# A hybrid decoder layer: two slabs of the first stage share a buffer, the squares are added in another order, and the table of slots is set anew

## The chip, the core and the metric

The kernel runs on one core of one Trainium2 chip. The core has TensorE (PE, matrix products; PEld is its load of the stationary operand), VectorE (DVE), ScalarE (ACT), GpSimd (POOL) and SyncE (SP, which here only issues DMAs). Each engine takes its own instructions in order and waits on semaphores for the others. The metric is the device time of one execution in microseconds, as the median of three runs.

## The reference, cut to what matters

The layer has 256 tokens of width 1024, in float32. It normalises x, projects it with one matrix, feeds two mixers (8 heads of block attention, 4 heads of a gated delta rule), and projects the result back onto x:

```
h    = rms_norm(x, norm_w)                         # mean of squares over 1024
proj = h @ w_in                                    # q,k,v,z of attention; qkv, z, b, a of the delta rule
qa, ka = rms_norm(heads(q_a)), rms_norm(heads(k_a))
y_a  = attention(qa, ka, v_a, rel_bias) * silu(z_a)
q_d, k_d, v_d = split(silu(causal_conv(qkv_dn)));  q_d, k_d = l2_norm(q_d), l2_norm(k_d)
g, beta = -exp(a_log) * softplus(a_dn + dt_bias), sigmoid(b_dn)
y_d  = rms_norm(gated_delta_rule_chunked(q_d, k_d, v_d, g, beta)) * silu(z_dn)
out  = x + concat(y_a, y_d) @ w_out
```

## The kernel before, in words

**Products.** Every large product is done in three passes: a float32 weight slab is split into a rounded part `wh` (ScalarE, line 188) and a rest `wl` (VectorE, line 189), x likewise into `xh` and `xl` (lines 259 and 260), and TensorE adds wh·xh, wh·xl and wl·xh (lines 249 to 251, 738 to 740, 827 to 829). The weights come as 44 slabs: z0 to z7 (128x520, the first stage), d0 to d11 (128x1024, inputs of the delta rule), then 16 slabs a (attention) and 8 slabs o (output). A slab is loaded by `load()` into one of four rotating buffers `wr` and split by `split()` into one of four `wh` and four `wl`. `chunk(i)` issues loads up to slab i+7 and splits up to slab i+4. All loads of slabs and of x (`px`, line 201) are issued by SP, in the order of the program.

**First stage.** Slab zk meets row block k of x; for each k there are two steps of six products. The mean of squares that the norm needs is made beside this in `norm()`: four squares of two row blocks each, `sq0` to `sq3` (ScalarE, line 269), added on VectorE (lines 274 and 276), then two small products with ones (line 279), which stand in TensorE's order between the two steps of k = 6. The result goes through `mtok` (line 281) and POOL (line 282) to `rtok`, for which the gates of the delta rule wait (line 302).

**Order of the work.** TensorE's order is the order in which the program is written: `products()` is the main stream, and after each of its steps `advance()` counts up by one and lets every other stream whose slot has come emit its next piece. The table `AT` holds these slots: ("base0", 1): 103 means that the second piece of stream base0 is emitted when the count is 103. The order on DVE, ACT, POOL and SP is made by a scheduler from priorities and its own estimate of the times, so a new slot moves instructions there too. The streams: `bias` (attention bias), `norm`, `gates`, `prep0` and `prep2` (delta rule heads, transposes L429, products L453 and L469), `base0` and `base1` (a triangular inverse: VectorE steps L498 and L500, transposes L503 and L507, products from L520 on), `scan0` to `scan3`, `heads..` (q and k of attention, L636 to L660), `pair0` to `pair3` (softmax of two heads: logits L680, maximum L687, exponential L123, division L698, transposes L703, values L714 and L716). L123 is the line of a helper that ScalarE's activations share, L135 that of the reciprocal root on POOL.

Of the kernel before, what the change touches and what calls it, by code (L numbers as in the profile page):

```python
# [8 lines left out]
F32 = mybir.dt.float32  # L9
F32R = mybir.dt.float32r  # L10
AF = mybir.ActivationFunctionType
ALU = mybir.AluOpType
AX = mybir.AxisListType

P = 128
S = 256
D = 1024
KT = 8
# [7 lines left out]
ZC = 520  # L26
# [8 lines left out]
LD, LS, PRI, REP, MTL, BDK = 7, 4, 100, 16, 1, 14  # L35
OUTS = ((0, 2), (0, 0), (1, 2), (1, 0), (0, 3), (1, 3), (0, 1), (1, 1))
AT = {
    ("attention", 0): 89, ("attention", 1): 92, ("attention", 2): 128, ("attention", 3): 113, ("attention", 4): 129,
# [3 lines left out]
    ("base1", 8): 124, ("bias", 0): 0, ("bias", 1): 3, ("bias", 2): 43, ("gates", 0): 24, ("gates", 1): 35,  # L42
# [13 lines left out]
}  # L56
SEGS = (2, 0, 1, 3)
# [4 lines left out]
def tile_hymba_layer(ctx: ExitStack, tc: tile.TileContext, xt, wz, wdn, wat, wout, rb, cst, oneh, out):  # L62
    nc = tc.nc
    PE, ACT, DVE, POOL = nc.tensor, nc.scalar, nc.vector, nc.gpsimd
# [4 lines left out]
    wp = ctx.enter_context(tc.tile_pool(name="wp", bufs=4))  # L69
# [4 lines left out]
    def new(shape, name, dt=F32):  # L74
        return cp.tile(shape, dt, name=name, tag=name)

    def rot(shape, name, tag, bufs=2, dt=F32):
        return rp.tile(shape, dt, name=name, tag=tag, bufs=bufs)
# [55 lines left out]
    def rsqrt(y, m):  # L134
        POOL.tensor_tensor(out=y, in0=m, in1=mhalf.to_broadcast(list(m.shape)), op=ALU.pow)  # L135
# [13 lines left out]
    for _ in range(NWARM):  # L149
# [11 lines left out]
    WB = 1024  # L161
# [1 line left out]
              + [(f"d{i}", wdn[i], 1024) for i in range(12)]  # L163
              + [(f"a{s}{i}", wat[4 * s + i], 1024) for hf in range(2) for s in SEGS for i in (2 * hf, 2 * hf + 1)]
              + [(f"o{mh}{n}", wout[4 * mh + n], 1024) for mh, n in OUTS])
    raws, halves, loads = [], [], []

    def parts(i, n):
        return [slice(0, n)] if i else [slice(0, S), slice(S, n)]

    def load():
        if len(raws) < len(chunks):
            name, src, n = chunks[len(raws)]
            t = wp.tile([P, WB], F32, name=f"wr_{name}", tag="wr", bufs=4)
            for r in parts(len(raws), n):
                i = nc.sync.dma_start(t[:, r], src[:, r])
            raws.append(t)
            loads.append(i)
# [13 lines left out]
    def chunk(i):  # L192
        while len(raws) < min(i + LD, len(chunks)):
            load()
        while len(halves) < min(i + LS, len(chunks)):
            split()
        return halves[i]

    for k in range(KT):
        r = slice(P_COLS + k * S if k else 0, P_COLS + (k + 1) * S)  # L200
        nc.sync.dma_start(px[:, r], xt[:, r])
        load()
# [60 lines left out]
    def norm():  # L263
        ps = yield from grab1()
        for i in range(4):
            sq = rot([P, 2, S], f"sq{i}", "k2", 4)
            xi = x[:, 2 * i:2 * i + 2, :]
            if i in SQA:
                ACT.activation(sq, xi, AF.Square)
            else:  # L270
                POOL.tensor_tensor(out=sq, in0=xi, in1=xi, op=ALU.mult)
            sqs.append(sq)
        for i, j in ((0, 1), (2, 3), (0, 2)):
            DVE.tensor_tensor(out=sqs[i], in0=sqs[i], in1=sqs[j], op=ALU.add)
        sq = sqs[0]
        DVE.tensor_tensor(out=sq[:, 0, :], in0=sq[:, 0, :], in1=sq[:, 1, :], op=ALU.add)
        yield W_NORM
        for c in range(2):
            PE.matmul(ps[:, c:c + 1], lhsT=sqs[0][:, 0, c * P:(c + 1) * P], rhs=ones[:, 0:1], start=True, stop=True)
        m = new([P, 2], "mtok")  # L280
        DVE.tensor_scalar(out=m, in0=ps[:, 0:2], scalar1=1.0 / D, scalar2=EPS, op0=ALU.mult, op1=ALU.add)
        rsqrt(rtok, m)
        done["rtok"] = 1
        POOL.tensor_scalar(out=rhalf, in0=rtok, scalar1=0.5, scalar2=None, op0=ALU.mult)
        POOL.tensor_scalar(out=emt, in0=m, scalar1=EPS, scalar2=None, op0=ALU.mult)
        yield W_NORM2
        for c in range(2):
            PE.matmul(ps[:, S + c * P:S + (c + 1) * P], lhsT=rtok[:, c:c + 1].to_broadcast([P, P]), rhs=ident, start=True,
                      stop=True)
        ACT.copy(rbc, ps[:, S:])  # L290
        free.append(ps)
        table[2] = 1
        convs()
    sqs = []
# [110 lines left out]
    def convs():  # L405
        while early and table[2]:
            conv(*early.pop(0))
# [326 lines left out]
    def products():  # L734
# [11 lines left out]
        for k in range(KT):  # L746
            xsplit(k)
            w = chunk(k)
            if k == CSK:
                after(nc.sync.dma_start(cs, cst[:, 0:3, :]), loads[KT - 1])  # L750
            if k == NS:
                start("norm", norm())
                advance()
            for c in range(2):
                gemm(zb[2][:, c * S:(c + 1) * S], (xh, xl), w, k, c, slice(0, S), k == 0 and c == 0, k == KT - 1 and c == 1)
            yield
            for c in range(2):
                gemm(zb[c][:, :264], (xh, xl), w, k, c, slice(S, ZC), k == 0, k == KT - 1)
            yield
# [96 lines left out]
    def grab1():  # L856
        while not free:
            yield
        return free.pop(0)
# [67 lines left out]
```

## Time and profile before

| | us |
|---|---|
| median of three runs | 168.35 (168.16 to 170.61) |
| the profiled execution, its own time | 168.06 |
| its span, first to last instruction | 166.3 |
| mean granted TensorE clock | 0.996 |
| TensorE busy | 156.0 (94%) |
| VectorE busy | 131.0 (79%) |
| ScalarE busy | 103.6 (62%) |

The parts of the page give busy times by engine, the span in 40 slices, DMA queues, the chain of work that ended last, and the costliest groups by line. A row of the timeline is: start, duration, engine, line, operation, output<-inputs, shape, count, and in brackets the idle time before it with what ended it. A row of the windows view gives for one stretch each engine's busy time, the granted clock, the busy share of the DMA engines and GB/s.

### The profile page before, as it was taken

Reading aid. Unit: us, or ns where it says so; the run is one execution under the profiler, and the core shown is the slowest. Engines: PE = TensorE matmul, PEld = TensorE weight load, DVE = VectorE, ACT = ScalarE, POOL = GpSimd, SP = SyncE. Lnnn points to the kernel's source line nnn. Section 1 sums busy time; section 2 is a strip of 40 time slices with the busy share of each in tenths; the row PEclk is TensorE's granted clock in tenths of the full one; section 3 lists DMA queues with packets and bytes.
Section 4 is the critical chain, followed back from the end, with each engine's and each line's share of the span. In section 5 each row is a group of like instructions: output and inputs, shape, how many; then the busy total and the mean of one; then the engine's idle time right before and its main releaser. Section 6 shows DMA issues by size and latency. Waiting matters only on the chain.

```text
span 166.3 us, 4037 instructions
## 1 busy us (share of the span) xinstructions
PE 156.0 (94%) x1548; PEld 146.8 (88%) x1548; DVE 131.0 (79%) x380; ACT 103.6 (62%) x244; POOL 21.1 (13%) x29
## 2 busy tenths in 40 slices
PE   7799699989999999999998999999999979999990
PEld 7589699989999999999997879988988857999990
DVE  2579689999399999989998999898675997357261
ACT  5688498538997468686645596744666885342200
POOL 7200160000002000033041001031121000003000
PEclk9999999999999999999999999999999999999998
DMA  5998988899746047674343433334223300000033
GB/s 131 278 328 248 342 283 249 253 205 187 312 140 236 7 167 238 229 229 158 126 124 128 132 126 126 132 130 130 54 84 118 126 0 0 4 0 0 4 126 126
DMA packets 9930, 25.01 MB, mean 150 GB/s; under 512 B 1165, under 2 KB 3981, under 8 KB 9912
## 3 DMA queue, kind: packets, MB, share of 16 engines
q1 hardware_dynamic: 9208, 23.66, 46.2%
q10 hardware_dynamic: 576, 0.92, 1.5%
q8 instruction: 12, 0.20, 0.5%
q0 software_dynamic: 128, 0.18, 0.4%
q14 instruction: 6, 0.05, 0.1%
HBM read 23.52 MB, written 1.25 MB: 149 GB/s over the span
## 4 chain that ended last, share of the span: by engine, by line
PE 55%; DVE 19%; ACT 10%; DMA 6%; issue 5%; SPq 2%; POOL 2%; ACTq 0%; DVEq 0%
PE ps L249 5%; PE ps L827 5%; PE ps L829 5%; PE ps L828 5%; PE ps L251 4%; PE ps L250 4%; PE ps L739 4%; PE ps L738 4%; PE ps L740 4%; DVE wl_d L189 3%; DMA px<-xt 3%; DMA wr_z<-wz 2%; DVE wl_a L189 2%; PE ps L703 2%; ACT wh_d L188 2%
## 5 line engine op out<-in xcount | busy, mean ns | idle before, releaser
L249 PE MATMUL ps<-wh_a,xh 128*128 128x256 f32 x96 | 28.4, 296 | 0.0
L738 PE MATMUL ps<-xh,wh_d 128*128 128x256 f32 x96 | 27.7, 289 | 0.0
L739 PE MATMUL ps<-xl,wh_d 128*128 128x256 f32 x96 | 26.8, 279 | 0.0
L740 PE MATMUL ps<-xh,wl_d 128*128 128x256 f32 x96 | 26.8, 279 | 0.0
L250 PE MATMUL ps<-wh_a,xl 128*128 128x256 f32 x96 | 26.7, 278 | 0.0
L251 PE MATMUL ps<-wl_a,xh 128*128 128x256 f32 x96 | 26.7, 278 | 0.0
L188 ACT CAST wh_a<-wr_a 128x1024 fp32r<-128x1024 f32 x16 | 16.8, 1052 | 8.8 <-PE ps L739 6.6
L189 DVE TENSOR_TENSOR wl_a<-wr_a,wh_a 128x1024 fp32r<-128x1024 f32 x16 | 19.5, 1221 | 0.7 <-ACT sqa L636 0.3
L398 DVE SCALAR_TENSOR_TENSOR cv<-un,px,cv 128x255 f32<-128x255 f32 (+2 forms) x36 | 16.8, 476 | 2.5 <-ACT cv L396 2.5
L827 PE MATMUL ps<-yh,wh_o 128*128 128x256 f32 x64 | 18.8, 293 | 0.0
L249 PEld LDWEIGHTS ps<-wh_a,xh 128*128 128x128 f32 x96 | 18.1, 188 | 0.7 <-issue 0.5
L250 PEld LDWEIGHTS ps<-wh_a,xl 128*128 128x128 f32 x96 | 18.1, 189 | 0.1
L738 PEld LDWEIGHTS ps<-xh,wh_d 128*128 128x128 f32 x96 | 18.1, 188 | 0.1
L739 PEld LDWEIGHTS ps<-xl,wh_d 128*128 128x128 f32 x96 | 18.0, 188 | 0.1
L251 PEld LDWEIGHTS ps<-wl_a,xh 128*128 128x128 f32 x96 | 18.1, 188 | 0.0
L740 PEld LDWEIGHTS ps<-xh,wl_d 128*128 128x128 f32 x96 | 18.0, 187 | 0.0
L829 PE MATMUL ps<-yh,wl_o 128*128 128x256 f32 x64 | 17.9, 279 | 0.0
L828 PE MATMUL ps<-yl,wh_o 128*128 128x256 f32 x64 | 17.9, 279 | 0.0
L189 DVE TENSOR_TENSOR wl_d<-wr_d,wh_d 128x1024 fp32r<-128x1024 f32 x12 | 14.7, 1221 | 1.8 <-ACT wh_d L188 1.8
L188 ACT CAST wh_d<-wr_d 128x1024 fp32r<-128x1024 f32 x12 | 12.7, 1056 | 4.1 <-DMA wr_d<-wdn 2.5
L189 DVE TENSOR_TENSOR wl_o<-wr_o,wh_o 128x1024 fp32r<-128x1024 f32 x8 | 9.8, 1221 | 4.5 <-ACT wh_o L188 4.4
L827 PEld LDWEIGHTS ps<-yh,wh_o 128*128 128x128 f32 x64 | 12.0, 188 | 0.5 <-issue 0.3
(209 smaller groups left out, 404.6 us busy)
## 6 DMA issues: line engine op xcount, KB each, us to landing
wr_a<-wat SPq DMA_DIRECT2D x16, 512.0 KB, 3.4
wr_d<-wdn SPq DMA_DIRECT2D x12, 512.0 KB, 5.5
wr_o<-wout SPq DMA_DIRECT2D x8, 512.0 KB, 3.3
wr_z<-wz SPq DMA_DIRECT2D x7, 260.0 KB, 4.1
T<-bd SPq DMA_DIRECT2D x8, 128.0 KB, 6.3
px<-xt SPq DMA_DIRECT2D x7, 128.0 KB, 4.0
out_t<-ot ACTq DMA_DIRECT2D x3, 256.0 KB, 2.4
cs<-cst SPq DMA_DIRECT2D x1, 192.0 KB
```

The costliest lines, as they stand in the source:

```text
L188: ACT.copy(h[:, r], raw[:, r])
L189: eng.tensor_tensor(out=l[:, r], in0=raw[:, r], in1=h[:, r].bitcast(F32), op=ALU.subtract)
L249: PE.matmul(ps, lhsT=xa, rhs=wh[:, cols], start=first, stop=False)
L250: PE.matmul(ps, lhsT=xb, rhs=wh[:, cols], start=False, stop=False)
L251: PE.matmul(ps, lhsT=xa, rhs=wl[:, cols], start=False, stop=last)
L398: DVE.scalar_tensor_tensor(out=a[:, 3 - j:], in0=src[:, 0:S - 3 + j], scalar=pr[:, o + j:o + j + 1], in1=a[:, 3 - j:], op0=ALU.mult, op1=A ...
L738: PE.matmul(ps, lhsT=w[0][:, wk], rhs=xh[:, k, :], start=first, stop=False)
L739: PE.matmul(ps, lhsT=w[0][:, wk], rhs=xl[:, k, :], start=False, stop=False)
L740: PE.matmul(ps, lhsT=w[1][:, wk], rhs=xh[:, k, :], start=False, stop=last)
L827: PE.matmul(ps, lhsT=w[0][:, o], rhs=yh[:, k, :], start=(first and j == 0 and (m % 2 == 0 or alone)), stop=False)
L828: PE.matmul(ps, lhsT=w[0][:, o], rhs=yl[:, k, :], start=False, stop=False)
L829: PE.matmul(ps, lhsT=w[1][:, o], rhs=yh[:, k, :], start=False, stop=(last and j == 1 and (m % 2 == 1 or alone)))
```

## The change

Three edits. In `load()`, the slabs z0 to z7 go in pairs into one buffer (z0 and z1, z2 and z3, and so on), so that the eight take the four buffers once and none has to wait until an earlier one is split. In `norm()`, the three sums of 512 columns and one of 256 become two of 512 and three of 256: `sq0` takes `sq1` and `sq2` whole, is then folded to 256 columns, and takes the two halves of `sq3` one by one. And 52 of the 95 entries of `AT` have other numbers; of this table one line stands here.

```diff
-    ("norm", 0): 13, ("norm", 1): 12, ("norm", 2): 18, ("pair0", 0): 101, ("pair0", 1): 112, ("pair0", 2): 118,
+    ("norm", 0): 13, ("norm", 1): 14, ("norm", 2): 18, ("pair0", 0): 101, ("pair0", 1): 112, ("pair0", 2): 118,
...
-    raws, halves, loads = [], [], []
+    raws, halves, loads, slabs = [], [], [], []
...
-            t = wp.tile([P, WB], F32, name=f"wr_{name}", tag="wr", bufs=4)
+            i = len(raws)
+            if i < KT:
+
+                if i % 2 == 0:
+                    slabs.append(wp.tile([P, 2 * ZC], F32, name=f"wr_{name}", tag="wr", bufs=4))
+                t = slabs[-1][:, i % 2 * ZC:(i % 2 + 1) * ZC]
+            else:
+                t = wp.tile([P, WB], F32, name=f"wr_{name}", tag="wr", bufs=4)
...
-        for i, j in ((0, 1), (2, 3), (0, 2)):
-            DVE.tensor_tensor(out=sqs[i], in0=sqs[i], in1=sqs[j], op=ALU.add)
+
         sq = sqs[0]
-        DVE.tensor_tensor(out=sq[:, 0, :], in0=sq[:, 0, :], in1=sq[:, 1, :], op=ALU.add)
+        for j in (1, 2):
+            DVE.tensor_tensor(out=sq, in0=sq, in1=sqs[j], op=ALU.add)
+        for o in (sq[:, 1, :], sqs[3][:, 0, :], sqs[3][:, 1, :]):
+            DVE.tensor_tensor(out=sq[:, 0, :], in0=sq[:, 0, :], in1=o, op=ALU.add)
```

On SP, in the first stage, before: the loads of z4 to z7 (`wr_z`), the blocks of x between them, and the first slabs d. The brackets name the semaphores waited for; DMAHW0 to DMAHW7 are those of the eight DMAs issued before.

```order
L176 DMA wr_z_112<-wz 128x520 [waits DMAHW2_49,DVE_49]
L201 DMA px<-xt 128x256 [waits DMAHW3_49]
L176 DMA wr_z_115<-wz 128x520 [waits DMAHW4_49,DVE_49]
L201 DMA px<-xt 128x256 [waits DMAHW5_49]
L176 DMA wr_z_118<-wz 128x520 [waits DMAHW6_49,DVE_49]
L201 DMA px<-xt 128x256 [waits DMAHW7_49]
L176 DMA wr_z_121<-wz 128x520 [waits DMAHW0_49,DVE_49]
L750 DMA cs<-cst 128x384 [waits DMAHW1_49]
L176 DMA wr_d_221<-wdn 128x1024 [waits DMAHW2_49,DVE_49]
```

The same place now (lines are those of the changed file):

```order
L183 DMA wr_z_110<-wz 128x520 [waits DMAHW2_49]
L208 DMA px<-xt 128x256 [waits DMAHW3_49]
L183 DMA wr_z_110<-wz 128x520 [waits DMAHW4_49]
L208 DMA px<-xt 128x256 [waits DMAHW5_49]
L183 DMA wr_z_115<-wz 128x520 [waits DMAHW6_49]
L208 DMA px<-xt 128x256 [waits DMAHW7_49]
L183 DMA wr_z_115<-wz 128x520 [waits DMAHW0_49]
L183 DMA wr_d_215<-wdn 128x1024 [waits DMAHW1_49,DVE_49]
L759 DMA cs<-cst 128x384 [waits DMAHW2_49]
```

The waits for VectorE are gone from z4 to z7; a wait for the landing of the eighth DMA before stays in every row. Slab d0 goes ahead of the constants `cs`.

On VectorE, the end of the first stage before (`xl` the rest of x, `wl_z5` to `wl_z7` the rests of slabs, `sq` the sums of squares, `mtok` the scaled mean):

```order
L189 TENSOR_TENSOR wl_z5_224<-wr_z5_115,wh_z5_223 128x520
L260 SCALAR_TENSOR_TENSOR xl_124<-px_96,xh_123 128x256
L189 TENSOR_TENSOR wl_z6_245<-wr_z6_118,wh_z6_244 128x520
L274 TENSOR_TENSOR sq2_304<-sq2_304,sq3_306 128x512
L189 TENSOR_TENSOR wl_z7_265<-wr_z7_121,wh_z7_264 128x520
L274 TENSOR_TENSOR sq0_300<-sq0_300,sq2_304 128x512
L276 TENSOR_TENSOR sq0_300<-sq0_300 128x256
L189 TENSOR_TENSOR wl_d0_285<-wr_d0_221,wh_d0_284 128x1024
```

And now:

```order
L283 TENSOR_TENSOR sq0_296<-sq0_296,sq2_300 128x512
L267 SCALAR_TENSOR_TENSOR xl_120<-px_96,xh_119 128x256
L196 TENSOR_TENSOR wl_z5_218<-wr_z4_110,wh_z5_217 128x520
L285 TENSOR_TENSOR sq0_296<-sq0_296 128x256
L196 TENSOR_TENSOR wl_z6_241<-wr_z6_115,wh_z6_240 128x520
L285 TENSOR_TENSOR sq0_296<-sq0_296,sq3_302 128x256
L196 TENSOR_TENSOR wl_z7_261<-wr_z6_115,wh_z7_260 128x520
L285 TENSOR_TENSOR sq0_296<-sq0_296,sq3_302 128x256
L196 TENSOR_TENSOR wl_d0_281<-wr_d0_215,wh_d0_280 128x1024
```

Behind `wl_z7` stood two dependent sums, of 512 and of 256 columns; now one of 256 stands there. (Rows of `xl` that only repeat are left out.)

On VectorE, the end of base0's steps before (`Mt` and `tm` its serial steps, `Mp` and `MT` its result, `Lb` the start of base1, `qn` and `zs` of attention, `wl_a` the rest of a slab):

```order
L646 TENSOR_TENSOR qn_1311<-ps_77,r_1309 128x512
L500 TENSOR_TENSOR Mt_155<-Mt_155,tm_852 128x2x2x2
L805 TENSOR_TENSOR zs_1364<-ps_76,rbc 128x512
L498 TENSOR_TENSOR tm_852<-Lb_850,Mt_155 128x4
L189 TENSOR_TENSOR wl_a_1372<-wr_a_1195,wh_a_1371 128x1024
L487 STREAM_TRANSPOSE Lb_1324<-pk_1319 128x512
L500 TENSOR_TENSOR Mt_155<-Mt_155,tm_852 128x2x2
L498 TENSOR_TENSOR tm_1326<-Lb_1324,Mt_156 128x2x15
L503 STREAM_TRANSPOSE Mp_883<-Mt_155 128x4x4x8
L500 TENSOR_TENSOR Mt_156<-Mt_156,tm_1326 128x2x15
L507 STREAM_TRANSPOSE MT<-Mp_883 32x4x32 x2
```

And now:

```order
L655 TENSOR_TENSOR qn_1341<-ps_78,r_1339 128x512
L509 TENSOR_TENSOR Mt_151<-Mt_151,tm_859 128x2x2x2
L507 TENSOR_TENSOR tm_859<-Lb_857,Mt_151 128x4
L814 TENSOR_TENSOR zs_1361<-ps_76,rbc 128x512
L509 TENSOR_TENSOR Mt_151<-Mt_151,tm_859 128x2x2
L496 STREAM_TRANSPOSE Lb_1277<-pk_1272 128x512
L512 STREAM_TRANSPOSE Mp_890<-Mt_151 128x4x4x8
L196 TENSOR_TENSOR wl_a_1369<-wr_a_1204,wh_a_1368 128x1024
L507 TENSOR_TENSOR tm_1279<-Lb_1277,Mt_152 128x2x15
L516 STREAM_TRANSPOSE MT<-Mp_890 32x4x32 x4
L509 TENSOR_TENSOR Mt_152<-Mt_152,tm_1279 128x2x15
```

The split `wl_a` that stood ahead of `Mp` now stands behind it. On TensorE the first products of base0 (L520) move with this, from 12 products behind the logits of pair0 and pair1 (L680) to 6 ahead of them. Other moves on TensorE that the prediction speaks of: the product of the bias (L372) goes from after 18 products of the first stage to after 36; the first transposes of prep0 (L429) go 24 products later; one L453 and one L469 of prep2 trade places with products of the main stream; near the end the logits of pair3 (L680) go ahead of the transposes of pair2 (L703).

More of the change, by code (lines that the diff above doesn't have):

```diff
@@ L37 @@
 AT = {
-    ("attention", 0): 89, ("attention", 1): 92, ("attention", 2): 128, ("attention", 3): 113, ("attention", 4): 129,
[3 rows of a table removed]
-    ("base1", 8): 124, ("bias", 0): 0, ("bias", 1): 3, ("bias", 2): 43, ("gates", 0): 24, ("gates", 1): 35,
[12 rows of a table removed]
+    ("attention", 0): 88, ("attention", 1): 97, ("attention", 2): 128, ("attention", 3): 117, ("attention", 4): 120,
[3 rows of a table added]
+    ("base1", 8): 124, ("bias", 0): 0, ("bias", 1): 6, ("bias", 2): 43, ("gates", 0): 29, ("gates", 1): 35,
[12 rows of a table added]
     ("scan3", 5): 211,
```

28 rows, old and new, of the table AT are left out of this document.

## The prediction

> **What bounds the kernel now.** I began with the page's first part and then asked who waits for whom on TensorE.
>
> ```profile
> PE 156.0 (94%) x1548; PEld 146.8 (88%) x1548; DVE 131.0 (79%) x380; ACT 103.6 (62%) x244; POOL 21.1 (13%) x29
> ...
> PE ps L703 <- DVE pb L698: 1.6, 3, 1.0
> PE ps L279 <- DVE sq L276: 1.4, 1, 1.4
> PE ps L654 <- DVE qn L646: 0.8, 1, 0.8
> PE ps L249 <- ACT wh_z L188: 0.7, 2, 0.4
> PE ps L354 <- DVE eD L347: 0.5, 1, 0.5
> ```
>
> TensorE is busy 156.0 of 166.3 us. The change takes no product away, so all it can save is idle time, and the five waits above (us in total, times, longest) sum to 5.0 us. More than 3 us is hard to reach: each wait would have to go without another coming. The second longest, 1.4 us, lies in the stage that the change names. The chain of waits around it:
>
> ```profile
> 11.69 3.98 DMA wr_z<-wz
> ...
> 15.77 0.64 ACT wh_z L188
> ...
> 17.14 0.61 DVE sq L274
> ...
> 17.77 0.44 DVE sq L276
> ```
>
> Columns are start and duration. The load of z7 is issued at 11.69 and lands at 15.7; then come its split on ScalarE and VectorE, two dependent sums of squares, and only then the product L279, for which the rest of TensorE's queue (half of k = 6, all of k = 7, the d slabs) stands in line. TensorE's rows there:
>
> ```profile
> 16.54 0.28 PE L251 MATMUL ps<-wl_z,xh 128*128 128x256 f32 x1
> 18.25 0.61 PE L279 MATMUL ps<-ones,sq 128*128 128x1 f32 x4 [1.43 <-DVE sq L276]
> ```
>
> Products start 0.12 us apart, so TensorE could have gone on at 16.66: 1.6 us are lost here.
>
> Later stages have another limit. In the windows view (stretch, length, then PE, PEld, DVE, ACT, POOL busy):
>
> ```profile
> 26.00:40.00 14.00, 13.45 (x116) 13.25 (x115) 14.00 (x41) 8.02 (x14) 0.00 (x0) 1.00 0.92 220
> ...
> 50.00:85.00 35.00, 35.00 (x294) 34.62 (x292) 33.94 (x98) 24.24 (x60) 4.12 (x3) 1.00 0.49 165
> ```
>
> From 26 to 40 VectorE is never idle, and from 50 to 85 TensorE and VectorE both are full. So a saving of TensorE's at 18 us lasts only if VectorE, too, gets ahead; if it doesn't, TensorE waits longer where it waits for VectorE now, at L354, L654 and L703.
>
> **The change part by part: the first stage.** ScalarE's and VectorE's rows from 10 us on, all back to back, give what each step occupies (start to next start):
>
> ```profile
> 10.76 0.50 ACT L259 ACTIVATE xh<-px 128x256 fp32r<-128x256 f32 x1
> 11.17 0.46 ACT L375 COPY V<-ps 8x384 f32<-8x384 f32 x1
> 11.53 0.62 ACT L188 CAST wh_z<-wr_z 128x520 fp32r<-128x520 f32 x1
> 12.05 0.63 ACT L269 ACTIVATE sq<-px 128x512 f32<-128x512 f32 x1
> 12.59 0.49 ACT L259 ACTIVATE xh<-px 128x256 fp32r<-128x256 f32 x1
> ...
> 10.58 0.48 DVE L260 SCALAR_TENSOR_TENSOR xl<-px,xh 128x256 fp32r<-128x256 f32 x1
> 10.97 0.69 DVE L189 TENSOR_TENSOR wl_z<-wr_z,wh_z 128x520 fp32r<-128x520 f32 x1
> 11.58 0.48 DVE L260 SCALAR_TENSOR_TENSOR xl<-px,xh 128x256 fp32r<-128x256 f32 x1
> 15.25 0.69 DVE L274 TENSOR_TENSOR sq<-sq,sq 128x512 f32<-128x512 f32 x1
> 15.85 0.48 DVE L260 SCALAR_TENSOR_TENSOR xl<-px,xh 128x256 fp32r<-128x256 f32 x1
> 26.26 0.42 DVE L394 TENSOR_TENSOR un<-ps,rbc 128x256 f32<-128x256 f32 x1
> 26.60 0.16 DVE L327 TENSOR_SCALAR rs<-ua 128x8 f32<-128x8 f32 x1
> ```
>
> ScalarE: split of a slab 0.52, `xh` 0.41, copy of the bias row 0.36, square 0.54. VectorE: split of a slab 0.61, `xl` 0.39, sum of 512 columns 0.60, of 256 columns 0.34 (from L394, the nearest 256-column sum).
>
> *Loads.* SP's rows, and the time to landing that the DMA view gives for z3 (issued 4.48):
>
> ```profile
> 4.48 0.43 SPq L176 DMA_DIRECT2D wr_z<-wz  x1
> wr_z<-wz SPq DMA_DIRECT2D x1, 260.0 KB, 5.4
> 12.91 10.91 SPq L176 DMA_DIRECT2D wr_d<-wdn  x7
> ```
>
> The order shows that z4 to z7 lose their wait for VectorE, but not the wait for the DMA eight places before. z7 then waits for z3's landing, 4.48 + 5.4 = 9.9, instead of 11.69, and with z7's own 4.0 us lands near 13.9 instead of 15.7. Slab d0, issued at 12.91 now, follows z7 near 10.4. All lie in one SP queue behind one another, so a later load does not hold up an earlier one by much; what remains is whether the engines can move more. The window 8 to 10 us shows the most that they moved in this stage:
>
> ```profile
> 8.00:10.00 2.00, 2.00 (x12) 1.22 (x12) 0.89 (x3) 1.32 (x3) 0.00 (x0) 1.00 1.05 373
> ```
>
> From z3's landing on, four slabs (260 KB) and four blocks of x (128 KB), 1.59 MB, have still to land by z7: 4.3 us at 373 GB/s, so z7 lands at 14.2 by rate. I keep 14.2. The Trainium skill (DMA: Bandwidth & Descriptors, Specifications) sets the share of one core in HBM at about 358 GB/s; by that the estimate is 4.4 us and 14.3. The trace's 373 is above it, and either time is ahead of the next limit:
>
> *ScalarE.* Its order is kept but for the bias copy, which moves from before z4's split to before `xh6`. From 11.17: split z4, square 2, `xh5`, split z5, copy, `xh6`, split z6, square 3, `xh7` end at 11.17 + 0.52 + 0.54 + 0.41 + 0.52 + 0.36 + 0.41 + 0.52 + 0.54 + 0.41 = 15.40; z7's split starts there (15.77 before) and ends at 16.0. So of z7's 1.5 us of earlier landing only 0.37 is of use.
>
> *VectorE.* From 11.58 with the new order: `xl4` 11.97, split z4 12.58, sum with square 2 13.18, `xl5` 13.57, split z5 14.18, fold 14.52, `xl6` 14.91, split z6 15.52, first half of square 3 15.86, `xl7` 16.25, split z7 16.86, and the last sum, 0.44 long, ends at 17.30. L279 starts near 17.35 instead of 18.25: **0.9 us**. Nearly all of it is the order of the sums: were z7 as late as now, the last sum would end at 17.14 + 0.44 and still save 0.65. TensorE stands at L279 from 16.66 as before, and still waits 0.7. The bias product moves to where `wl_z3` is awaited anyway, and is worth nothing.
>
> One more sum is issued, of the same 1792 columns in all. The Trainium skill (VectorE: DVE Perf Modes, Rules for kernel authors) says to minimise the count of chained VectorE operations, since each drains the pipeline whatever it does; by that rule alone the stage would lose one fixed cost, and the saving would be about 0.8. The rows bear the cost out (0.34 for 256 columns against 0.60 for 512), and it lies ahead of the last sum, where the list above has it already.
>
> **From 18 to 50 us.** `wl_d0` follows the last sum at 17.3, since d0 lands by 15.6 (512 KB behind z7, 1.4 us at 373 GB/s). So `mtok`, and the gates behind it, come earlier too, but line 302 also needs the end of k = 7, which is 0.9 earlier. VectorE's set of steps up to `eD` (the wait at L354) is the same within one step of 0.3, so it comes 0.6 to 0.9 earlier, and TensorE's saving passes L354 at about 0.9. The transposes L429 of prep0 go 24 and 6 products later, which leaves ScalarE more time for what they read; I cost that at nothing.
>
> **From 50 to 100 us.** VectorE carries the same work in another order. The chain there, then TensorE's rows:
>
> ```profile
> 85.37 2.68 POOL r L135
> ...
> 88.08 0.69 DVE qn L646
> ...
> 91.51 0.22 DVE Mp L503
> ...
> 93.34 0.29 DVE pb L687
> ...
> 93.98 1.14 DVE wl_a L189
> ```
>
> ```profile
> 91.48 1.58 PE L680 MATMUL ps<-kT,qT 64*128 64x128 f32 x16
> 94.60 0.44 PE L520 MATMUL ps<-Mp,LT 32*32 32x16 f32 x32
> 99.00 1.16 PE L703 MATMUL ps<-cs,pb 128*128 128x128 f32 x6 [0.38 <-DVE pb L698]
> ```
>
> Base0 comes a little later at first (one `wl_a`, 1.14 us, goes ahead of it) and earlier at the end (another goes behind `Mp`).
>
> VectorE's lead on itself decides L654 (waits for `qn`) and L703 (waits for `pb`). I bound it by 0.6 (what it has at 26 us, less one step) and 1.4 (if d and a slabs, split earlier, leave it no holes till 85); TensorE's saving after L703 is then 0.6 to 1.3, and I take 0.9, the value at which it entered. L520 now stands 18 products of 0.12, and the logits' 1.5 us, further ahead: 94.60 - 2.2 - 1.5, or 90.9 on the old clock. `Mp` was ready at 91.51 + 0.22 and loses the 1.14 us of `wl_a` from before it: 90.6. No wait, by 0.3 us.
>
> **The end.** The logits of pair3 go earlier on TensorE, but the maximum L687 stands behind a split of 1.2 us on VectorE in both versions:
>
> ```profile
> 132.86 1.21 DVE L189 TENSOR_TENSOR wl_o<-wr_o,wh_o 128x1024 fp32r<-128x1024 f32 x1
> 134.88 0.25 ACT v L611
> ```
>
> so only ScalarE's `v` (0.25), which leaves the middle of the four exponentials, is won: 0.2 us off the wait at L703.
>
> Sum: 0.9 carried through, 0.2 at the end, **1.1 us** off the profiled execution's own 168.06: 166.95. The median of the runs shown is 0.29 above that execution; with half of it the forecast is **167.1**.
>
> **Rivals.**
> - *The saving grows.* VectorE's lead reaches 1.4 us and the waits at L654 and L703 (0.8 and 0.38) go as well, with 0.2 more of L354's: 1.1 + 1.4 = 2.5 us, 165.7. For it: every slab is split earlier. Against: POOL's 2.68 us at 85.37 are not touched. Chance 0.17.
> - *The saving is eaten.* VectorE, full from 26 to 40 and from 50 to 85, is not ahead by 50 us, and TensorE waits longer at L654. Only the 0.2 at the end is left: 168.1. Chance 0.2.
> - *Slower.* L520 is reached before `Mp` is there. The `wl_a` that goes ahead of base0 holds `Mp` back 1.14 us, the one behind it is waited for elsewhere, and TensorE stands at L520, with the logits of pair0 and pair1 behind it, which now come after. The logits start as now (91.48) if `Mp` is there by 91.0; from then on each 1 us costs one, since VectorE takes them up at 93.34 with little room. With `Mp` 1.14 later than now, less the saving's 0.9, it comes at 91.73 + 1.14 - 0.9 = 92.0, and costs 1.0; with the 0.15 to the median, 169.2. It decides if VectorE has no lead at 90 us. Chance 0.08.
> - *The loads don't come earlier*, since the wait for the eighth DMA takes the place of the one removed. Then the order of sums alone works, 0.65 + 0.2: 167.4. The order speaks for the wait, z3's landing at 9.9 against its mattering. Chance 0.05.
>
> **How the numbers follow.** My forecast has 0.5. Its own range is 166.6 to 167.8 (saving 0.6 + 0.0 to 1.3 + 0.2, and the 0.29 between execution and median). The range for 8 in 10 takes in the eaten saving and most of the grown one: **165.4 to 168.9**; left out are the slower case and the lower half of the grown one. Two per cent is 3.4 us, about what a measurement of this kernel can tell from no change: faster than 165.0 needs more than the grown case (0.06), slower than 171.7 three times the slower one (0.03), so 0.91 lies within.
>
> **What would show it.** Right: z7's load issued near 9.9, its split on ScalarE without a wait for a DMA, L279 starting 0.7 to 1.1 earlier with VectorE's last sum ending its wait; TensorE's L354, L654 and L703 each reached and left about 0.9 earlier. Wrong: L279 not before 18; or L654 left at 88.8 as now (eaten); or a wait of TensorE for `Mp` at L520 (slower). A wait that is in no row of before, such as a PSUM bank whose reader now comes late, would make all of it wrong.

## The result, and the profile after

The changed kernel takes 165.63 us (median of 4 runs, 164.85 to 166.23). Beside the kernel before on the same chip the ratio is 0.9845, with a 95% interval of 0.9806 to 0.9883: 2.6 us less, by the interval 2.0 to 3.3. The forecast was 167.1 (1.1 us less), its range 165.4 to 168.9. The time lies in the range and on the forecast side, but where the rival "the saving grows" stood (165.7): the saving is more than twice the 1.1 us of the forecast, and the range held because it took in most of that rival. The profiled execution took 166.0 us, its span is 164.1 (166.3 before).

Busy times of the changed kernel, and who waits for whom on TensorE (us in total, times, longest):

```profile
PE 156.8 (96%) x1548; PEld 148.3 (90%) x1548; DVE 130.3 (79%) x381; ACT 103.1 (63%) x244; POOL 19.8 (12%) x29
...
PE ps L712 <- DVE pb L707: 1.2, 2, 0.9
PE ps L150 <- DVE ones L139: 1.0, 1, 1.0
PE ps L288 <- DVE sq L285: 0.5, 1, 0.5
PE ps L258 <- DVE wl_z L196: 0.4, 2, 0.2
```

TensorE, VectorE and ScalarE do about what they did; POOL is busy 1.3 us less. Gone are the waits for `qn` (0.8), for `eD` (0.5) and for ScalarE's `wh_z` (0.7); the one at the norm's product (L279 before, L288 now) fell from 1.4 to 0.5, and of the three for `pb` (1.6 in all) the first, 0.38 us near 98 us, is gone.

Where TensorE gained is read by comparing the start of the same product in both profiled executions. Each row below gives, for one kernel, the start minus that of the kernel before, in us; lines are those before. E1 to E12 are the experiments of the next section.

| kernel | norm L279 | gates L354, 2nd | prep0 L429, 4th pair | prep2 L429, 2nd head | qn L654, 2nd | pb L703, first | L703, pair3 | span |
|---|---|---|---|---|---|---|---|---|
| before, start | 18.25 | 36.88 | 47.77 | 71.56 | 88.82 | 99.00 | 137.09 | 166.3 |
| **changed** | -0.66 | -1.07 | -0.28 | -1.02 | -1.74 | -2.11 | -2.41 | -2.2 |
| E1 pairs | +0.41 | +0.12 | +0.13 | +0.09 | +0.09 | +0.08 | +0.08 | +0.1 |
| E2 sums | -1.11 | -0.25 | +1.13 | +1.09 | +0.13 | -0.06 | +0.07 | +0.1 |
| E3 slots | -0.48 | +0.12 | +0.92 | +0.17 | -0.60 | +0.10 | -0.08 | -0.1 |
| E4 pairs, sums | -1.11 | -1.45 | -0.06 | -0.11 | -1.06 | -1.25 | -1.13 | -0.3 |
| E5 one row moved | -0.57 | -0.42 | -0.40 | -0.44 | -1.40 | -1.48 | -1.60 | -1.6 |
| E6 E4 and gates slots | -1.26 | -1.56 | -0.59 | -0.89 | -0.78 | -1.24 | -1.37 | -1.4 |
| E7 without gates slots | -0.67 | -1.40 | -1.58 | +0.11 | +0.02 | -0.33 | -0.52 | -0.3 |
| E8 without pairs | -1.38 | -0.89 | -0.09 | -1.13 | -1.89 | -2.20 | -2.51 | -2.3 |
| E9 pairs, same order | -0.71 | -1.41 | +0.38 | +0.38 | +0.38 | +0.38 | +0.26 | +0.2 |
| E10 E6, one row moved | -0.90 | -1.22 | +0.09 | -0.42 | -0.88 | -1.33 | -1.45 | -1.5 |
| E11 norm later | -0.59 | +0.31 | +1.00 | +0.03 | -0.60 | +0.08 | -0.23 | -0.2 |
| E12 old end slots | -1.06 | -1.78 | -1.09 | -2.13 | -2.70 | -3.08 | -3.09 | -2.8 |

(Prep0's products stand at another place of the queue in some of them; prep2's are the safer column.) In the changed kernel 0.7 us enter at the norm, 0.4 come at L354, then nothing up to 72 us, and 0.7 come at L654 and 0.4 at L703. These are about the waits that the rival counted (0.8 at L654, 0.38 at L703, 0.2 of the one at L354).

How far a single profile can be read is shown by E12. Up to 128 us TensorE, VectorE and ScalarE have the same order in it as in the changed kernel, and yet it stands 0.40 us further ahead at the norm, 1.11 at prep2 and 0.97 at the first L703. What comes at L654 and L703 is alike in both (0.72 and 0.37 in the changed kernel, 0.57 and 0.38 in E12); what comes before is not.

The first stage, TensorE's, ScalarE's and VectorE's rows, and SP's row of z7 with its time to landing from the DMA view:

```profile
17.59 0.61 PE L288 MATMUL ps<-ones,sq 128*128 128x1 f32 x4 [0.54 <-DVE sq L285]
...
15.65 0.61 ACT L195 CAST wh_z<-wr_z 128x520 fp32r<-128x520 f32 x1
...
16.51 0.69 DVE L196 TENSOR_TENSOR wl_z<-wr_z,wh_z 128x520 fp32r<-128x520 f32 x1
17.12 0.41 DVE L285 TENSOR_TENSOR sq<-sq,sq 128x256 f32<-128x256 f32 x1
...
10.32 0.33 SPq L183 DMA_DIRECT2D wr_z<-wz  x1
...
wr_z<-wz SPq DMA_DIRECT2D x1, 260.0 KB, 4.1
```

z7 lands at 10.32 + 4.1 = 14.4; its split starts at 15.65 and no DMA ends the idle time before it; one sum of 0.41 us stands behind `wl_z7`.

And the place at 85 us, POOL's power and VectorE's rows around it, before:

```profile
85.37 2.67 POOL L135 TENSOR_TENSOR r<-s,mhalf 128x8 f32<-128x8 f32 x1 [6.73 <-DVE s L641]
...
85.13 0.17 DVE L641 SCALAR_TENSOR_TENSOR s<-s,emt 128x8 f32<-128x8 f32 x1
85.21 0.18 DVE L500 TENSOR_TENSOR Mt<-Mt,tm 128x16 f32<-128x16 f32 x1
85.32 1.23 DVE L189 TENSOR_TENSOR wl_a<-wr_a,wh_a 128x1024 fp32r<-128x1024 f32 x1
```

and in the changed kernel:

```profile
83.87 1.64 POOL L135 TENSOR_TENSOR r<-s,mhalf 128x8 f32<-128x8 f32 x1 [5.01 <-DVE s L650]
...
83.62 0.17 DVE L650 SCALAR_TENSOR_TENSOR s<-s,emt 128x8 f32<-128x8 f32 x1
83.71 0.17 DVE L509 TENSOR_TENSOR Mt<-Mt,tm 128x16 f32<-128x16 f32 x1
83.92 0.18 DVE L507 TENSOR_TENSOR tm<-Lb,Mt 128x12 f32<-128x12 f32 x1
84.13 0.17 DVE L509 TENSOR_TENSOR Mt<-Mt,tm 128x12 f32<-128x12 f32 x1
84.29 1.23 DVE L196 TENSOR_TENSOR wl_a<-wr_a,wh_a 128x1024 fp32r<-128x1024 f32 x1
```

The same power of 128x8 takes 1.64 us instead of 2.67. Before, the split `wl_a` stood one small step (`Mt`) behind the scaled sum `s` and had started 0.05 us ahead of the power; now two more small steps stand between, and the power has started when the split does.

### The profile page after: what moved, and what is told of

Its sections match the earlier page's. It is cut to its first block, busy times and chain, and to the rows that moved or that the text cites. A ratio compares the mean times of both kernels' runs of the same rounds, so it can differ in the third digit from the quotient of the medians.

```text
span 164.1 us, 4034 instructions
## 1 busy us (share of the span) xinstructions
PE 156.8 (96%) x1548; PEld 148.3 (90%) x1548; DVE 130.3 (79%) x381; ACT 103.1 (63%) x244; POOL 19.8 (12%) x29
## 3 DMA queue, kind: packets, MB, share of 16 engines
HBM read 23.52 MB, written 1.25 MB: 151 GB/s over the span
## 4 chain that ended last, share of the span: by engine, by line
PE 70%; DVE 13%; ACT 6%; DMA 3%; issue 2%; SPq 2%; POOL 1%; DVEq 0%
PE ps L256 8%; PE ps L257 7%; PE ps L258 7%; PE ps L748 6%; PE ps L749 6%; PE ps L747 6%; PE ps L836 4%; PE ps L838 4%; PE ps L837 4%; DVE wl_d L196 3%; DMA px<-xt 3%; PE ps L462 2%; DVE cv L407 2%; PE ps L689 1%; PE ps L712 1%
## 5 line engine op out<-in xcount | busy, mean ns | idle before, releaser
L748 PE MATMUL ps<-xl,wh_d 128*128 128x256 f32 x96 | 26.8, 280 | 0.0
L748 PEld LDWEIGHTS ps<-xl,wh_d 128*128 128x128 f32 x96 | 18.1, 188 | 0.1
```

The costliest lines, as they stand in the source:

```text
L748: PE.matmul(ps, lhsT=w[0][:, wk], rhs=xl[:, k, :], start=False, stop=False)
```

## The experiments

**The three parts alone, and two together (E1 to E4).** The theory of the prediction, A: the saving enters at the sums and grows or shrinks by VectorE's lead. The rival, B: the larger part is the power near 85 us.

E1, the pairs alone:

```diff
...
+                if i % 2 == 0:
+                    slabs.append(wp.tile([P, 2 * ZC], F32, name=f"wr_{name}", tag="wr", bufs=4))
+                t = slabs[-1][:, i % 2 * ZC:(i % 2 + 1) * ZC]
```

> Only the paired slab buffers are added to the kernel before; sums and slots are the old ones. Theory A (the saving enters at the sums of squares, and what comes later grows from VectorE's lead): z7 lands near 14.4 instead of 15.7, its split on ScalarE starts near 15.4, but two dependent sums still stand behind it, so the product L279 starts near 17.9, 0.3 us earlier; the waits for qn (0.8) and pb stay; total about 0.3 us less, 0.998. Theory B (the larger part is the wait for qn near 88 us: POOL's power takes 2.67 us there because a wide VectorE split starts just ahead of it, and it takes 1.64 where two small steps stand between): on VectorE the split stands as before directly behind the scaled sum, so the power takes 2.67 again and the wait for qn stays: also about 0.3 us less. A and B agree here.

Measured: 1.006 (1.0024 to 1.0095), slower, which neither theory had. VectorE's rows, and TensorE's:

```profile
16.46 0.68 DVE L281 TENSOR_TENSOR sq<-sq,sq 128x512 f32<-128x512 f32 x1
17.07 1.21 DVE L196 TENSOR_TENSOR wl_d<-wr_d,wh_d 128x1024 fp32r<-128x1024 f32 x1
18.20 0.41 DVE L283 TENSOR_TENSOR sq<-sq 128x256 f32<-128x256 f32 x1
...
18.66 0.49 PE L286 MATMUL ps<-ones,sq 128*128 128x1 f32 x3 [1.72 <-DVE sq L283]
```

The sum of 512 columns ended in time, but the new program order has `wl_d0` (1.21 us) between it and the fold, and L279 starts later than before.

E2, the sums alone:

```diff
+        for j in (1, 2):
+            DVE.tensor_tensor(out=sq, in0=sq, in1=sqs[j], op=ALU.add)
+        for o in (sq[:, 1, :], sqs[3][:, 0, :], sqs[3][:, 1, :]):
+            DVE.tensor_tensor(out=sq[:, 0, :], in0=sq[:, 0, :], in1=o, op=ALU.add)
```

> Only the new order of the sums of squares is added to the kernel before. By its program order, the split wl_a then stands two small steps further behind the scaled sum near 85 us, without any new slot. Theory A: L279 0.65 us earlier (17.6), the wait for qn shrinks only as far as VectorE's lead grows, total 0.65 less, 0.996. Theory B: 0.65 at L279, and the power near 84 us takes 1.64 us instead of 2.67, so that the wait of 0.8 us for qn is gone: total about 1.5 to 1.8 us less, 0.990.

Measured: 0.9983 (0.9954 to 1.0013). L279 came 1.11 us earlier in its profile, more than the 0.65 of the text (E5, with the old sums, has 0.57 there, so a part of it need not be the edit's). The wait for `qn` was gone as B had it. But TensorE waited 0.6 us for `g` and 0.6 for `eD` near 35 us and 1.4 for `kq` near 48 us, and nothing was left. Both theories missed that.

E3, the table alone:

```diff
-    ("gates", 0): 24, ("gates", 1): 35,
+    ("gates", 0): 29, ("gates", 1): 35,
...
-    ("prep0", 3): 38, ("prep0", 4): 40, ("prep0", 5): 36, ("prep0", 6): 50, ("prep0", 7): 62, ("prep0", 8): 73,
+    ("prep0", 3): 38, ("prep0", 4): 42, ("prep0", 5): 24, ("prep0", 6): 36, ("prep0", 7): 53, ("prep0", 8): 68,
...
```

> Only the new table of slots is set in the kernel before; buffers and sums are the old ones. Theory A: L279 stays at 18.25, VectorE has no lead, only 0.2 us at the end is won: 0.2 less, 0.999. Theory B: the split stands two small steps behind the scaled sum, so the power takes 1.64 us, the wait for qn is gone although nothing came earlier in the first stage: 0.8 to 1.2 us less, 0.994.

Measured: 0.9971 (0.9945 to 0.9997). The power took 1.64 us and the wait for `qn` was gone, as B says, but others came. TensorE's waits in E3:

```profile
PE ps L354 <- DVE eD L347: 0.9, 1, 0.9
PE ps L520 <- DVE Mp L503: 0.8, 1, 0.8
```

The wait at L520 for `Mp` is the mechanism of the prediction's rival "slower", with nearly its price (0.8 for 1.0): the slots alone bring it, and in the changed kernel, where VectorE is ahead, it is not among the waits.

E4, the edits of E1 and E2 together, with the old table:

> The whole change but with the old table of slots. Theory A: L279 0.66 us earlier as in the changed kernel (17.6), grown to 0.9 or 1.1 at L354; without the new slots nothing at the end; 0.9 to 1.1 less, 0.994. Theory B: the power near 84 us takes 1.64 us here too (the split stands behind two small steps), the wait for qn is gone: 1.7 to 2.0 us less, 0.989; the new slots would then be worth only the last few tenths.

Measured: 0.9955 (0.9927 to 0.9982), less gain than either had, though A's 0.994 lies in the interval. L279 is 1.11 earlier, L354 1.45, and then the gain is gone at the transposes of `kq`. TensorE's wait, and ScalarE's rows there:

```profile
PE ps L438 <- ACT kq L123: 1.4, 1, 1.4
...
46.04 1.04 ACT L195 CAST wh_d<-wr_d 128x1024 fp32r<-128x1024 f32 x1 [0.18 <-PE ps L748]
...
47.25 0.41 ACT L123 ACTIVATE kq<-cv 128x256 f32<-128x256 f32 x1
```

ScalarE was 1.3 us ahead at `zd` near 41 us (40.27 against 41.58), but makes this `kq` at 47.25, as late as before (47.31). Its order now has one more split of a d slab ahead of `kq`, the one at 46.04, which had waited 0.18 us for a buffer that TensorE's own L748 frees; in the kernel before that split comes behind `kq`, at 48.01. (E2 has the same split there, at 47.24.) So `kq` does not come forward with TensorE's queue, and the second group of transposes, which stands 6 products earlier in it than in the changed kernel, waits. Between 72 us and L654 0.95 us come back, with a power of 1.64.

Together: the three parts alone give 1.006, 0.9983 and 0.9971, and all three 0.9845. The saving is in none of them; each alone, and E4, runs into a wait that the changed kernel does not have. None of them is one edit alone, either: the scheduler moved 13 of VectorE's rows in E1, 66 in E2 and E4 and 75 in E3, so what a part is worth by itself can't be read from these runs.

**The power (E5).** Theory B by itself, in the kernel before: one instruction of VectorE is moved, by a dependency that the scheduler keeps and that is no wait on the chip.

```diff
...
+            if len(halves) == 30:
+                rest.append(i)
...
+            if gq == 0 and r == 12:
+                step.append(i)
+                if rest:
+                    after(rest[0], i)
```

> The kernel before with one VectorE instruction moved: the split wl_a that stood directly behind the scaled sum near 85 us now stands two small steps (tm, Mt) further back; nothing else differs on any engine. Theory B (POOL's power is held until a wide VectorE split that started just ahead of it has ended): the power near 85 us takes 1.64 us instead of 2.67, the wait of 0.8 us for qn is gone, and the wait of 0.38 for pb at 98 us shrinks as well: 0.8 to 1.2 us less, 0.993 to 0.995. Rival (the length of the power has nothing to do with the split, or what is won is lost again at 98 us, where VectorE decides): power 2.67 as before, or the wait for pb 0.8 longer; 1.000.

Measured: 0.9932 (0.9896 to 0.9969), as B says. The power in E5, and TensorE's first wait for `pb`:

```profile
84.93 1.64 POOL L135 TENSOR_TENSOR r<-s,mhalf 128x8 f32<-128x8 f32 x1 [6.73 <-DVE s L651]
...
97.52 1.16 PE L713 MATMUL ps<-cs,pb 128*128 128x128 f32 x6 [0.36 <-DVE pb L708]
```

The wait for `qn` is gone. One part of B's expectation failed: the wait for `pb` near 98 us did not shrink (0.36 against 0.38).

The 0.6 us by which L279 is earlier in its profile is not the edit's, since the program up to there is the same (the loads landed earlier in that execution). From L354 (-0.42) to L703 (-1.48) it wins 1.06 us, which agrees with the ratio (0.68% of 168 us, 1.1 us). So moving one split behind two steps of 0.17 us is worth 1.1 us in the kernel before. The changed kernel with the split put back was not run.

**The gates' slots (E6, E7).** In the table, the four entries of the gates, of which three differ, put the transposes of `kq` behind 288 and 294 products instead of 264 and 288. (They are set on one line here.)

```diff
-    ("gates", 0): 24, ("gates", 1): 35, ("gates", 2): 33, ("gates", 3): 45,
+    ("gates", 0): 29, ("gates", 1): 35, ("gates", 2): 29, ("gates", 3): 49,
```

E6 adds them to E4. E7 takes them out of the changed kernel, where the transposes then stand behind 264 and 270 products:

> Buffers and sums as in the change, the old table but for the four new slots of the gates; on TensorE these put the transposes of kq behind 288 and 294 products of the d slabs instead of 264 and 288. Theory C (the slots are worth the wait for kq: in the experiment with buffers and sums alone TensorE stood 1.37 us there, since it had come forward and ScalarE's split of a d slab had not): the wait of 1.37 us near 46 us is gone and does not come back, 0.9955 becomes 0.987 to 0.989. Rival D (from 50 to 85 us VectorE decides): TensorE waits later for what it gained, 0.994 to 0.996.

> The whole change but with the four old slots of the gates; the transposes of kq stand behind 264 and 270 products of the d slabs. Theory C: a wait of about 1.4 us for kq comes back, the ratio rises from 0.9845 to about 0.992. Rival D: 0.985 to 0.987.

Measured: E6 0.9934 (0.9904 to 0.9963), E7 0.9993 (0.9955 to 1.0032). E6 is nearer to D than to C, and its 0.2% against E4 is within both intervals. The wait for `kq` fell from 1.4 to 0.5, but the scheduler's order had put a split one small step behind the scaled sum again:

```profile
84.61 2.66 POOL L116 TENSOR_TENSOR r<-s,mhalf 128x8 f32<-128x8 f32 x1 [5.05 <-DVE tm L488]
...
PE ps L644 <- DVE qn L636: 0.8, 1, 0.8
```

so the wait for `qn` stayed as in the kernel before. What the transposes gave (at 72 us E6 is 0.89 ahead, E4 0.11) E4 makes up at L654, where its power is not held; at L703 both stand at -1.25. E6 has no wait for `pb` near 98 us, although its power is held; E5 has one, although its power is not. E7 lost more than C had, all that the change gives:

```profile
PE ps L419 <- ACT kq L104: 1.9, 1, 1.9
...
PE ps L644 <- DVE qn L636: 0.9, 1, 0.9
```

TensorE was 1.40 us ahead at L354 and 0.11 behind at 72 us. That L654 then waits for `qn`, though its power took 1.64, was not foreseen. POOL's row and VectorE's rows ahead of `qn` show the reason:

```profile
84.87 1.64 POOL L116 TENSOR_TENSOR r<-s,mhalf 128x8 f32<-128x8 f32 x1 [5.87 <-DVE Mt L490]
...
85.61 1.18 DVE L177 TENSOR_TENSOR wl_a<-wr_a,wh_a 128x1024 fp32r<-128x1024 f32 x1
86.71 0.19 DVE L488 TENSOR_TENSOR tm<-Lb,Mt 128x30 f32<-128x30 f32 x1
86.82 1.24 DVE L497 STREAM_TRANSPOSE MT<-Mp 32x128 f32<-32x128 f32 x4
88.10 0.69 DVE L636 TENSOR_TENSOR qn<-ps,r 128x512 f32<-128x512 f32 x1
```

The power is done at 86.51, but VectorE's order has a split and four transposes `MT` ahead of `qn`. 69 of VectorE's rows moved against the changed kernel, so E7 shows that the change needs these slots as its order now is, but does not split the 1.5% between the wait for `kq` and that order.

**Both in one (E10).** E6 with the split near 84.6 us moved one small step (`Mt`) back, so that two stand between it and the scaled sum; the expectation's "two small steps later" is one too many.

```diff
...
+            if gq == 0 and r == 13:
+                step.append(i)
+                if rest:
+                    after(rest[0], i)
```

> The kernel with pairs, sums and the four gates slots, and one VectorE instruction moved: the split wl_a near 84.6 us two small steps later, nothing else on any engine. Theory B and C together: in the kernel without the move the power took 2.66 there and TensorE waited 0.75 us for qn; now 1.64 and no wait: 0.9934 becomes 0.987 to 0.990, most of what the whole change gives (0.9845). Rival (VectorE decides at 98 us anyway): 0.993.

Measured: 0.9913 (0.988 to 0.9947). The power is 1.64 us again, but the wait for `qn` only halves (0.4), since other steps of VectorE stand ahead of `qn` in this order. Against E6 that is 0.2%, within both intervals. It lies between the expectation of 0.987 to 0.990 and the rival's 0.993, and its interval holds both. What the change's other slots add beyond E10 (0.7%, with intervals that just touch) was not taken apart.

**The loads (E8, E9).** E8 is the changed kernel without the pairs:

```diff
-                if i % 2 == 0:
-                    slabs.append(wp.tile([P, 2 * ZC], F32, name=f"wr_{name}", tag="wr", bufs=4))
-                t = slabs[-1][:, i % 2 * ZC:(i % 2 + 1) * ZC]
+            t = wp.tile([P, WB], F32, name=f"wr_{name}", tag="wr", bufs=4)
```

> The whole change without the paired slab buffers (each slab waits for a buffer again). Theory: the pairs are not worth anything at L279, which the order of the sums decides (17.1 us both with and without them in the two experiments with the new sums), but they bring the d slabs, and with them the power of the norm, 1.7 us earlier, on which the gates and the waits at L345 and L354 (0.58 and 0.60 us with the new sums alone) hang: about 1.0 us of the saving is lost, 0.990 to 0.992. Rival (the new slots cover it, or the loads are limited by rate anyway): 0.985 to 0.987.

Measured: 0.9894 (0.9851 to 0.9938). That is 0.5% above the changed kernel, but the intervals overlap (that one ends at 0.9883), so a loss is not shown, and this one holds the theory and the rival both. Nor do the profiles show the 1.0 us of the theory. With the pairs (the changed kernel) the norm's power starts 1.3 us earlier, at 18.82 and not 20.14, but it then takes 1.74 us, in E8 0.73 (see the last section). L354 differs by only 0.18 us, and the spans are 164.1 with the pairs and 164.0 without. (15 rows on VectorE and 8 on ScalarE moved with this edit.) E9 is E1 with `wl_d0` held behind the fold, so that only the loads differ from the kernel before:

```diff
...
+            if len(halves) == 8:
+                rest.append(i)
...
+        step.append(i)
+        if rest:
+            after(rest[0], i)
```

> Only the paired buffers, and one more dependency that keeps the split wl_d0 behind the last fold of the squares, so that TensorE, ScalarE, VectorE and POOL have the very order of the kernel before and only the loads differ. In the experiment with the pairs alone VectorE did wl_d0 between the last two sums, and L279 started at 18.66 instead of 18.25. Theory: that row is what made the pairs alone slower; without it the last fold ends near 17.4, L279 starts at 17.3 to 17.7, and the power near 85 us is still held (2.67), the wait for qn still 0.8: 0.996 to 0.999. Rival (earlier d slabs themselves disturb something later): 1.003 to 1.006 as with the pairs alone.

Measured: 0.9927 (0.9895 to 0.996), better than expected. Against E1 only the order differs (13 rows on VectorE, with `wl_d0` the first of them, and 4 on ScalarE), and that is worth 1.3% (1.006 to 0.9927). The profiled execution of E9 took 168.45 us, against a median of 167.04; L354 is 1.41 earlier in it, and it shows how the loads can spoil that:

```profile
45.97 1.04 ACT L197 CAST wh_d<-wr_d 128x1024 fp32r<-128x1024 f32 x1 [1.66 <-DMA wr_d<-wdn]
...
PE ps L445 <- ACT kq L123: 1.8, 1, 1.8
```

A d slab landed late, and `kq` and the transposes waited behind its split. How the 0.7% reaches the end in the other executions this profile does not show, and whether the changed kernel's places for the transposes bear such a slab better was not tested.

**The wait that is left at the norm (E11).** One more slot is moved in the changed kernel:

```diff
-    ("norm", 0): 13, ("norm", 1): 14, ("norm", 2): 18
+    ("norm", 0): 13, ("norm", 1): 15, ("norm", 2): 18
...
```

> The whole change with one more slot: the second step of norm at 15 instead of 14, so that six products of k = 6 stand ahead of L279 (288 in the changed file), where TensorE now waits 0.54 us. If what enters in the first stage is carried through (the main case of the forecast), 0.5 us more is won: 0.981 to 0.982. If VectorE decides from 26 us on, the wait moves to L354: 0.984 to 0.986. VectorE's program order near 85 us keeps two small steps between the scaled sum and the split.

Measured: 0.9983 (0.9943 to 1.0024), worse than either. The wait at the norm is gone, but 65 rows of VectorE moved, and two more splits of d slabs came ahead of the gates' `g` (34.83 instead of 30.55), the later of them directly. VectorE's rows and TensorE's wait:

```profile
33.68 1.23 DVE L177 TENSOR_TENSOR wl_d<-wr_d,wh_d 128x1024 fp32r<-128x1024 f32 x1 [0.40 <-ACT wh_d L176]
34.83 0.16 DVE L326 TENSOR_TENSOR g<-ln,eal 128x8 f32<-128x8 f32 x1
...
PE ps L333 <- DVE g L326: 1.7, 1, 1.7
```

A step of 0.16 us waits for ScalarE's split (0.40) and VectorE's (1.15), and TensorE 1.7 us for it; `Mp` then is late again (0.8 at L520).

**The end (E12).** The changed kernel with the old slots of attention, the pairs 2 and 3 and the scans:

```diff
-    ("pair2", 0): 111, ("pair2", 1): 148, ("pair2", 2): 151,
+    ("pair2", 0): 126, ("pair2", 1): 140, ("pair2", 2): 153,
...
```

> The whole change but with the old slots of attention, pair2, pair3 and scan0 to scan3; nothing differs ahead of 105 us but the order from there to the end. The forecast put the worth of these slots at 0.2 us, from ScalarE's v at L611 that leaves the exponentials: the ratio rises from 0.9845 by about 0.001. Rival (the end decides more than that, since the wait of 0.9 us for pb there is the longest left): 0.988 to 0.990.

Measured: 0.9805 (0.976 to 0.9849), the lowest of all. Its interval overlaps the changed kernel's, so that it beats that one is not shown; nor do the times show the 0.2 us that the prediction gave the new end slots. From the first L703 to pair3's the changed kernel wins 0.30 us (-2.11 to -2.41) and E12 0.01; at the end of the span the changed kernel has given 0.2 back, E12 0.3. E12's profile also has no wait at the norm or at L354: the slabs landed early in it, and what entered, 1.06 us there and 1.78 at L354, was still there at the end.

## Why the prediction was right, and where it was wrong

- **What bounds the kernel** was right: TensorE is as busy as before, all of the saving is waits, and it stayed under the 3 us that the text called hard to pass (2.6, by the interval up to 3.3). The list of waits left out one of 1.0 us (L150, for `ones`), which the change does not touch, and the eaten case sums to 168.0, not 168.1.
- **Loads.** z7 was issued at 10.32 (9.9 in the text) and landed at 14.4 (14.2), held by the eighth DMA before it, as said. z7's split started at 15.65 without a wait for a DMA (15.40).
- **L279.** 17.59 against 17.35, 0.66 us earlier against 0.9. TensorE waited 0.54 there (0.7 in the text). With the same new sums E2, E4, E8 and E12 have 1.1 to 1.4. But executions of one program differ there by 0.4 (the changed kernel and E12) to 0.6 (the kernel before and E5), so the profiles agree with the term and can't size it more closely.
- **"Nearly all of it is the order of the sums"** holds at L279, of which it was said (E2 and E4 both -1.11), and not for the time: the pairs, with the order on the computing engines kept, win 0.7% (E9). With them the d slabs and the gates come earlier (L354 -0.25 in E2, -1.45 in E4). The prediction saw the earlier d slabs and let line 302's need of k = 7 cancel them. That the changed kernel would lose without the pairs is not shown (E8).
- **"I cost that at nothing"**, of the transposes L429, is the first step that failed. They are not a gain in themselves (E3); they help to keep the gain: 1.4 us went there in E4, 1.9 in E7. The text looked at what the later place gives ScalarE, and not at the wait that comes at an earlier place when TensorE arrives 1.4 us earlier and `kq` does not. What made `kq` late differs: one more split ahead of it in ScalarE's order (E4), a late d slab (E9); in E7 it came 1.6 us earlier than before (45.73), and TensorE earlier still.
- **"POOL's 2.68 us at 85.37 are not touched"**, the argument against the rival that came true, is the second. The row had been read as the price of the operation, though the same operation takes 1.64 elsewhere in the same trace; 1.03 us of it was a hold, and the order put that aside. With it went the wait for `qn`; L654 and L703 were left 1.74 and 2.11 us earlier, not the 0.9 that the text named as its sign. The wait for `pb` near 98 us, which the rival counted too, is gone, but not by the power (E5 keeps it, E6 is without it). So the growth from 0.9 to 2.1 was rightly priced (1.4 for the rival) and for its largest part wrongly reasoned: not every slab's earlier split, but one split's place. That the time lies in the range, which took in this rival at a chance of 0.17, is luck in that sense: the price was there, the mechanism was not.
- **"No wait, by 0.3 us" at L520** held in the changed kernel, and the rival "slower" has its mechanism (0.8 us in E3 and E11), where L354 is 0.1 and 0.3 us late; having no lead is the condition that the prediction gave it. It is not enough: E7 has no lead at 72 us either and no such wait, since its order makes `Mp` at 85.4.
- **The end:** 0.3 us at L703 as forecast (0.2), but no gain in the time is shown (E12).
- What stays open: which of the other slots make up the 0.7% between E10 and the change, what takes away the wait for `pb` near 98 us, and what the pairs are worth in the changed kernel.

## What to carry to other kernels

A saving upstream lasts only if every later wait on the queue's way has its producer move with it: go through the products that follow and ask which of them is fed by work that hangs on another engine's order, a buffer or a DMA and not on the saving. Where small steps and wide ones share an in-order engine, read which wide step stands directly ahead of each small one that somebody waits for; here the place of one split was worth 0.7% (E5), and an order that began with one 1.3% (E1 against E9), more than any of the edits alone. And when one row of a trace takes longer than its like elsewhere in the trace, ask what ran beside it before taking it as a price.

## What the runs showed of the hardware

POOL's power is held by a wide VectorE step that has started ahead of it. In the 14 profiles the power of 128x8 occurs 56 times. In 39 no split was running at its start, and it took 1.63 to 1.64 us; in 17 one was, and it took 2.48 to 2.71: in each of the 17 the excess is what was left of the split less 0.14 to 0.15 us. The rows of the changed kernel at 109 us, POOL's and VectorE's:

```profile
108.95 2.48 POOL L135 TENSOR_TENSOR r<-s,mhalf 128x8 f32<-128x8 f32 x1 [9.25 <-DVE s L650]
...
108.72 1.22 DVE L196 TENSOR_TENSOR wl_o<-wr_o,wh_o 128x1024 fp32r<-128x1024 f32 x1
```

The split ends at 109.94, 0.99 us behind the power's start; 0.99 - 0.15 + 1.64 = 2.48. The Trainium skill (SBUF — State Buffer, SBUF: two separate sides) says that VectorE and GpSimd share a pair of ports under an exclusive lock, that whichever starts first, a VectorE step with two SBUF inputs (against a GpSimd step that reads SBUF) or a GpSimd step, takes it for the whole instruction, and that the other fully blocks. Where the split starts first the runs agree: the splits have two SBUF inputs, the power reads `s` from SBUF, and the hold lasts to the split's end. In the other direction the runs differ from the page and show no block: 24 splits started while such a power was running, 0.14 us or more behind its start, and took 1.18 to 1.23 us, as the others do (median 1.22). What happens to one that starts sooner no run here shows.

The norm's power, which makes the `rtok` that the gates wait for, is held in the same way. It took 0.73 us in the kernel before, and in the changed kernel:

```profile
18.82 1.74 POOL L135 TENSOR_TENSOR rtok<-mtok,mhalf 128x2 f32<-128x2 f32 x1 [13.75 <-DVE mtok L290]
...
18.75 1.23 DVE L196 TENSOR_TENSOR wl_d<-wr_d,wh_d 128x1024 fp32r<-128x1024 f32 x1
```

So here the earlier d slabs cost 1.0 us of what they bring. In E12, with the same order there, the split started only at 18.96, behind the power's start at 18.56, and the power took 0.73 again: whether a step is held can depend on when a load lands.

The second thing is the spread of the loads: with the same program up to there (the kernel before and E5) z7's split differed by 0.8 us and the product L279 by 0.6 between two executions, the changed kernel and E12 by 1.1 at 72 us, and a late d slab cost 1.8 us in E9's profile. A difference of this size in a single profile need not be the edit's.
